# A two-block network on one NeuronCore: the memory loaded whole into two tiles at the outset, the input right behind it and normalised ahead of the first products, and twelve products of a constant at the very start

## The chip, the cores and the metric

The kernel runs on one core of one Trainium2 chip, and the other cores are idle. The metric is the device time of one execution in microseconds (us). Inputs lie in HBM when it starts, and the output is back in HBM when it ends.

## The reference, cut to what matters

Two network blocks run one after the other on a sequence of 256 tokens of width 1024, all in float32. The first block has a gated short convolution, an MLP, a latent attention and a second MLP; each of its norms is modulated by a shift and a scale that come from a product of a vector `c` with the large matrix `ada_w`. The second block has a recurrent and an attention mixer, a cross attention over a memory of 256 rows, and an MLP. What the change touches is the cross attention's keys and values, and the first norm of the first block:

```python
# second block, cross attention: needs the memory alone, so the kernel computes it first
mem_n = rms_norm(mem, norm_mem)           # mem [1, 256, 1024]
k = mem_n @ w_xk                          # [256, 1024] x [1024, 1024]
v = mem_n @ w_xv
# first block, first norm
mod = silu(c) @ ada_w[0] + ada_b[0]       # shift, scale, gate, ...
h = rmsnorm(x, norm_g[0, 0]) * (1 + scale) + shift
bcx = h @ conv_in_w                       # [256, 1024] x [1024, 3072]
```

## The kernel before, in words

**How a product is made.** Every float32 operand is split in a high part (`hi`, rounded by ScalarE to the format that TensorE multiplies in one pass) and a low part (`lo = x - hi`, by VectorE). One logical product is three TensorE products: high by high, high by low, low by high (`mm3`, lines 236 to 238, with the weights stationary and 256 tokens moving; `mm3t`, lines 243 to 245, with the tokens stationary and 512 columns moving). Weights come in pieces of 512 KB, 128 x 1024 floats. `load` (line 212) fetches one by SyncE's DMA queue into one of 7 buffers of the pool `raw`; `split` (lines 216 and 217) makes `whi` on ScalarE and `wlo` on VectorE, after which the buffer is free again. So a load can be issued only when VectorE is done with the piece seven loads before it.

**Modulations as background.** `ada_step(n)` (line 331) loads 512 KB of the transposed `ada_w`, also into a `raw` buffer, and multiplies it on VectorE with the row `cb` (silu of `c`, spread over the partitions by eight transposes and two ScalarE copies, lines 305 and 306), summing along the row. Each `split` calls `background()`, which hands out such steps at a fixed rate for the stage. The first stage has 16 of these steps and four calls of `first_h` (lines 650 to 660), which make the modulated input `h` of the first block, two of its eight feature tiles a call.

**The first stage** (lines 591 to 687) computes the keys and values of the memory, so that TensorE has work while the modulations of the first block are made:

- For each of four quarters of the memory: load 256 KB of the transposed memory into `memT`, a tile of the pool `tmp` (7 tiles, which `memg` and `sqm` also use), load a piece of `w_xk` (lines 598, 599), scale the memory by the norm's gain into `memg` (line 602, two ScalarE copies of 128 x 256), split `memg` into `hmh` and `hml`, split the weights, and square the memory into `sqm` for the norm (line 606), added up on VectorE in `sqs` (lines 612, 614).
- The first half of the keys: 96 products of 256 columns into two PSUM tiles `us` (lines 615 to 621). Then the sums of squares by float32 products with a constant tile `ones` (`fmm`, line 248), the reciprocal roots `rm` and `rmc` (lines 626 to 634), and `memK` (line 639).
- The input `x`: two loads of 512 KB (line 678), and `first_x` (lines 662 to 670) for each 128 tokens: squares on ScalarE, `rstd`, two scaled copies `xs`, eight transposes on TensorE (line 669), two copies to `xn`. `first_h` reads `xn`.
- The second half of the keys (`up`, line 681), 96 products of 256 columns; then the values in two halves (lines 682 to 687), each 48 products of 512 columns and two ScalarE evacuations `memV`.

Then the convolution's input product begins, with `h` as its moving operand and pieces of `conv_in_w`.

**What sets the order.** The order of instructions on each engine and on SyncE's DMA queue is fixed when the program is built, by a list scheduler that goes by the order of the code and by its own estimate of when operands are there. On the chip each engine runs its list strictly in order, and waits where an operand isn't there yet.

Of the kernel before, what the change touches and what calls it, by code (L numbers as in the profile page):

```python
# [12 lines left out]
AF = mybir.ActivationFunctionType  # L13
# [22 lines left out]
TAIL = 6  # L36

# [49 lines left out]
def net(ctx, tc, t, out):  # L87
# [30 lines left out]
    def tmp(name, *shp):  # L118
        return shaped(tmpp.tile([P, 512], F32, name=name, tag="t"), shp)
# [203 lines left out]
    nc.sync.dma_start(ident, t["consts"][:, :128])  # L323
    cb = row(cact)
# [269 lines left out]
    mem, ws, sqa = [], [], None  # L594
    gm = vcol("norm_mem_2", 0, 8)
    for i in range(4):
        v = tmp("memT", 2, S)
        nc.sync.dma_start(v, t["memT"][i])
        raw = load(t["w_xk_2"][i])
        vg = tmp("memg", 2, S)  # L600
        for j in range(2):
            nc.scalar.activation(vg[:, j, :], v[:, j, :], AF.Copy, scale=gm[:, 2 * i + j:2 * i + j + 1])
        split_into(hm.ks(0, 2 * i, 2), hm.ks(1, 2 * i, 2), vg)
        ws.append(split(raw, 2, 512))
        q = tmp("sqm", 2, S)
        nc.scalar.activation(q, v, AF.Square)
        if i == 0:
            sqa = q
        else:
            if i == 1:  # L610
                sqs = big("sqs", 2, S)
                nc.vector.tensor_add(sqs, sqa, q)
            else:
                nc.vector.tensor_add(sqs, sqs, q)
    us = [utile() for _ in range(2)]
# [30 lines left out]
    xn = [big("xn", 4, S) for _ in range(2)]  # L646
# [15 lines left out]
    def first_x(tt):  # L662
        r = x_rstd(tt)
        for hf in range(2):
            v = tmp("xs", 512)
            nc.scalar.activation(v, xt[tt][:, hf, :], AF.Copy, scale=r)
            m = mtile()
            for j in range(4):
                nc.tensor.transpose(m[:, j * P:(j + 1) * P], v[:, j * P:(j + 1) * P], ident)
            nc.scalar.activation(xn[hf][:, :, tok(tt)], shaped(m, [4, P]), AF.Copy)  # L670

    for j in range(0, KT, 2):
        for n in (8 + j, j, 9 + j, j + 1):
            steps.append(((0, 0), lambda n=n: ada_step(n)))
        steps.append(((0, 0), lambda j=j: first_h(j)))
    pace["rate"] = len(steps) / MEM_PIECES
    for tt in range(2):
        nc.sync.dma_start(xt[tt], t["x"][tt * P:(tt + 1) * P, :].rearrange("p (a b) -> p a b", a=2))
    for tt in range(2):
        first_x(tt)  # L680
# [638 lines left out]
```

## Time and profile before

| | |
|---|---|
| median of 3 runs | 1044.45 us |
| lowest and highest | 1042.36 and 1044.8 us |
| the profiled execution's own time | 1044.24 us |
| its span | 1042.4 us |
| TensorE busy (matmul) | 998.4 us, 96% |
| VectorE busy | 735.2 us, 71% |
| ScalarE busy | 564.2 us, 54% |
| DMA | 231 MB, 222 GB/s mean |

The span is that of the instructions; the execution's own time holds 1.84 us more, around it. All times within the profile count from the start of the span. "PE" is TensorE, "PEld" its weight loads, "DVE" VectorE, "ACT" ScalarE, "SPq" SyncE's queue of DMA issues. A row of the timeline gives start, length, engine, line and operation, output and inputs, a count, and in brackets how long the engine had been idle just before and what ended that wait; rows of one kind that follow each other are merged. A row of products may overlap the next one, since products are pipelined: their pace is read from start to start.

### The profile page before, as it was taken

Reading aid. Unit: us, or ns where it says so; the run is one execution under the profiler, and the core shown is the slowest. Engines: PE = TensorE matmul, PEld = TensorE weight load, DVE = VectorE, ACT = ScalarE, POOL = GpSimd, SP = SyncE. Lnnn points to the kernel's source line nnn. Section 1 sums busy time; section 2 is a strip of 40 time slices with the busy share of each in tenths; the row PEclk is TensorE's granted clock in tenths of the full one; section 3 lists DMA queues with packets and bytes.
Section 4 is the critical chain, followed back from the end, with each engine's and each line's share of the span. In section 5 each row is a group of like instructions: output and inputs, shape, how many; then the busy total and the mean of one; then the engine's idle time right before and its main releaser. Section 6 shows DMA issues by size and latency. Waiting matters only on the chain.

```text
span 1042.4 us, 15822 instructions
## 1 busy us (share of the span) xinstructions
PE 998.4 (96%) x6090; PEld 871.8 (84%) x6090; DVE 735.2 (71%) x1108; ACT 564.2 (54%) x920; POOL 1.0 (0%) x8
## 2 busy tenths in 40 slices
PE   6979989999999979989999999999999999999997
PEld 5869977898888768667999988898878888998886
DVE  6878996898888589938866553868767556655542
ACT  6644446744435683868544453755556446444442
POOL 0000000000000000000000000000000000000000
PEclk9989989999999999998999999999999999999999
DMA  9788994798989369904976564573434336566611
GB/s 345 283 316 310 340 362 165 278 379 335 339 306 358 118 205 348 312 26 173 331 237 208 184 185 157 182 241 119 122 102 167 137 129 225 187 187 184 193 49 41
DMA packets 64731, 231.00 MB, mean 222 GB/s; under 512 B 7184, under 2 KB 7568, under 8 KB 64656
## 3 DMA queue, kind: packets, MB, share of 16 engines
q1 hardware_dynamic: 64512, 229.86, 63.3%
q8 instruction: 48, 0.79, 0.3%
q14 instruction: 27, 0.22, 0.1%
q10 hardware_dynamic: 144, 0.12, 0.0%
HBM read 228.91 MB, written 1.05 MB: 221 GB/s over the span
## 4 chain that ended last, share of the span: by engine, by line
PE 84%; DVE 6%; ACT 6%; DMA 2%; issue 1%; SPq 0%; ACTq 0%
PE acc L243 11%; PE acc L244 11%; PE acc L245 11%; PE u L236 10%; PE u L237 10%; PE u L238 10%; PE u L245 4%; PE u L244 4%; PE u L243 4%; PE m L248 3%; DVE wlo L217 2%; DVE raw L331 2%; ACT whi L216 1%; PE u L248 1%; PE acc L248 1%
## 5 line engine op out<-in xcount | busy, mean ns | idle before, releaser
L217 DVE TENSOR_TENSOR wlo<-raw,whi 128x1024 fp32r<-128x1024 f32 (+1 forms) x317 | 380.4, 1212 | 150.9 <-ACT whi L216 148.3
L216 ACT ACTIVATE whi<-raw 128x1024 fp32r<-128x1024 f32 (+1 forms) x317 | 327.7, 1048 | 225.9 <-PE u L237 89.8
L236 PE MATMUL u<-hh,whi 128*128 128x256 f32 x960 | 272.0, 283 | 2.7 <-ACT whi L216 2.7
L238 PE MATMUL u<-hh,wlo 128*128 128x256 f32 x960 | 271.8, 283 | 0.8 <-DVE wlo L217 0.8
L237 PE MATMUL u<-hl,whi 128*128 128x256 f32 x960 | 271.5, 283 | 0.0
L236 PEld LDWEIGHTS u<-hh,whi 128*128 128x128 f32 x960 | 182.0, 190 | 5.1 <-ACT whi L216 3.1
L237 PEld LDWEIGHTS u<-hl,whi 128*128 128x128 f32 x960 | 182.0, 190 | 1.9 <-issue 1.0
L238 PEld LDWEIGHTS u<-hh,wlo 128*128 128x128 f32 x960 | 181.8, 189 | 2.0 <-issue 1.0
L243 PE MATMUL acc<-whi,mh 128*128 128x512 f32 x384 | 151.7, 395 | 0.0
L244 PE MATMUL acc<-whi,ml 128*128 128x512 f32 x384 | 151.4, 394 | 0.0
L245 PE MATMUL acc<-wlo,mh 128*128 128x512 f32 x384 | 151.3, 394 | 0.0
L331 DVE SCALAR_TENSOR_TENSOR raw<-raw,row 128x1024 f32<-128x1024 f32 x112 | 136.1, 1219 | 5.5 <-DMA raw<-in_adaT_dram 5.4
L245 PEld LDWEIGHTS acc<-wlo,mh 128*128 128x128 f32 x384 | 72.3, 188 | 16.7
L244 PEld LDWEIGHTS acc<-whi,ml 128*128 128x128 f32 x384 | 72.3, 188 | 15.7
L243 PEld LDWEIGHTS acc<-whi,mh 128*128 128x128 f32 x384 | 72.2, 188 | 15.7
L243 PE MATMUL u<-whi,hh 128*128 128x512 f32 x144 | 59.5, 413 | 4.9 <-ACT hh L454 4.9
L244 PE MATMUL u<-whi,hl 128*128 128x512 f32 x144 | 59.4, 413 | 0.5 <-DVE hl L455 0.4
L245 PE MATMUL u<-wlo,hh 128*128 128x512 f32 x144 | 58.4, 406 | 0.0
L513 ACT ACTIVATE rl<-u 128x512 f32<-128x512 f32 x36 | 21.1, 586 | 35.1 <-PE u L238 35.1
L243 PEld LDWEIGHTS u<-whi,hh 128*128 128x128 f32 x144 | 27.9, 194 | 11.8 <-ACT hh L454 5.6
L475 DVE TENSOR_TENSOR rq<-rl 128x512 f32<-128x512 f32 x36 | 24.7, 686 | 14.3 <-ACT rl L513 14.2
L244 PEld LDWEIGHTS u<-whi,hl 128*128 128x128 f32 x144 | 28.1, 195 | 7.2 <-DVE hl L455 1.3
(318 smaller groups left out, 1241.3 us busy)
## 6 DMA issues: line engine op xcount, KB each, us to landing
raw<-in_adaT_dram SPq DMA_DIRECT2D x112, 512.0 KB, 5.4
raw<-in_mlp_up_w_dram SPq DMA_DIRECT2D x64, 512.0 KB, 5.1
raw<-in_mlp_down_w_dram SPq DMA_DIRECT2D x64, 512.0 KB, 4.7
raw<-in_w_ff_dram SPq DMA_DIRECT2D x64, 512.0 KB, 3.6
raw<-in_w_in_dram SPq DMA_DIRECT2D x28, 512.0 KB, 3.8
raw<-in_conv_in_w_dram SPq DMA_DIRECT2D x24, 512.0 KB, 4.9
raw<-in_w_xk_dram SPq DMA_DIRECT2D x8, 512.0 KB, 7.8
raw<-in_w_xv_dram SPq DMA_DIRECT2D x8, 512.0 KB, 5.7
```

The source lines that it names most:

```text
L216: nc.scalar.activation(hi, view, AF.Copy)
L217: nc.vector.tensor_sub(lo, view, f32(hi))
L236: nc.tensor.matmul(o, wh, xh, start=start, stop=False, skip_group_check=True)
L237: nc.tensor.matmul(o, wh, xl, start=False, stop=False, skip_group_check=True)
L238: nc.tensor.matmul(o, wl, xh, start=False, stop=stop, skip_group_check=True)
L243: nc.tensor.matmul(o, xh, wh, start=start, stop=False, skip_group_check=True)
L244: nc.tensor.matmul(o, xl, wh, start=False, stop=False, skip_group_check=True)
L245: nc.tensor.matmul(o, xh, wl, start=False, stop=stop, skip_group_check=True)
L248: nc.tensor.matmul(o, a, b, start=start, stop=stop, skip_group_check=True)
L331: nc.vector.scalar_tensor_tensor(raw, raw, 1.0, cb, op0=OP.mult, op1=OP.mult, accum_out=mods[:, n:n + 1])
L475: nc.vector.tensor_mul(q, h_, h_)
L513: nc.scalar.activation(r, pair(u), AF.Relu)
```

## The change

The memory gets two tiles of its own in the pool `bigp` (21 tiles of 128 x 1032 floats), half of it in each. Its four loads and those of the first four pieces of `w_xk` are issued in the code right after that of `ident`. Next in the code stand twelve float32 products of `ones` by itself, 128 x 128, into a PSUM tile that nothing reads; then the row `cb`. In the first stage the two loads of `x` stand ahead of everything, and `first_x` ahead of the first products of the keys. The gain is applied straight into `hmh` by ScalarE (two copies of 128 x 256 a quarter), and the low part is one VectorE instruction for each 128 x 256, (memory x gain) - high; `memg` is gone. The list `first_ada` gives the modulation steps in the same order as before.

```diff
+WARM = 12
...
     nc.sync.dma_start(ident, t["consts"][:, :128])
+    memt = [big("memT", 4, S) for _ in range(2)]
+    memv = [memt[i // 2][:, 2 * (i % 2):2 * (i % 2) + 2, :] for i in range(4)]
+    raws = []
+    for i in range(4):
+        nc.sync.dma_start(memv[i], t["memT"][i])
+        raws.append(load(t["w_xk_2"][i]))
+    warm = atile(3)
+    for i in range(WARM):
+        fmm(warm[:, :P], ones, ones, True, True)
     cb = row(cact)
...
+    first_ada = [n for j in range(0, KT, 2) for n in (8 + j, j, 9 + j, j + 1)]
+    for tt in range(2):
+        nc.sync.dma_start(xt[tt], t["x"][tt * P:(tt + 1) * P, :].rearrange("p (a b) -> p a b", a=2))
+    ws, sqa = [], None
     gm = vcol("norm_mem_2", 0, 8)
     for i in range(4):
-        v = tmp("memT", 2, S)
-        nc.sync.dma_start(v, t["memT"][i])
-        raw = load(t["w_xk_2"][i])
-        vg = tmp("memg", 2, S)
+        v = memv[i]
         for j in range(2):
-            nc.scalar.activation(vg[:, j, :], v[:, j, :], AF.Copy, scale=gm[:, 2 * i + j:2 * i + j + 1])
-        split_into(hm.ks(0, 2 * i, 2), hm.ks(1, 2 * i, 2), vg)
-        ws.append(split(raw, 2, 512))
+            k = 2 * i + j
+            nc.scalar.activation(hm.k(0, k), v[:, j, :], AF.Copy, scale=gm[:, k:k + 1])
+            nc.vector.scalar_tensor_tensor(hm.k(1, k), v[:, j, :], gm[:, k:k + 1], f32(hm.k(0, k)),
+                                           op0=OP.mult, op1=OP.subtract)
+        ws.append(split(raws[i], 2, 512))
...
+    xn = [big("xn", 4, S) for _ in range(2)]
+
+    def first_x(tt):
...
+    for tt in range(2):
+        first_x(tt)
     us = [utile() for _ in range(2)]
...
-    for tt in range(2):
-        nc.sync.dma_start(xt[tt], t["x"][tt * P:(tt + 1) * P, :].rearrange("p (a b) -> p a b", a=2))
-    for tt in range(2):
-        first_x(tt)
     up([t["w_xk_2"][4 + i] for i in range(4)], hm, memk_evac(1))
```

## Rows read from the trace of the kernel before

**Rows 1.** Part 1 of the page (busy time, share of the span, instructions of TensorE).
```profile
PE 998.4 (96%) x6090; PEld 871.8 (84%) x6090; DVE 735.2 (71%) x1108; ACT 564.2 (54%) x920; POOL 1.0 (0%) x8
```
**Rows 2.** Windows: for each stretch its length, then busy time and instructions of PE, PEld, DVE, ACT and POOL, the granted clock as a share of full speed, the DMA engines' share and GB/s.
```profile
50.00:60.00 10.00, 8.22 (x27) 5.96 (x28) 8.57 (x14) 6.66 (x9) 0.00 (x0) 0.83 1.02 399
60.00:80.00 20.00, 16.54 (x95) 14.66 (x94) 13.63 (x23) 8.31 (x12) 0.00 (x0) 0.91 0.81 284
76.00:140.00 64.00, 64.00 (x545) 63.90 (x544) 58.92 (x90) 29.09 (x37) 0.00 (x0) 1.00 0.92 332
```
**Rows 3.** Timeline of TensorE up to the first product of the values: the transposes of `c`, then products of the keys.
```profile
4.12 1.97 PE L305 MATMUL m<-ident,cact 128*128 128x128 f32 x8 [4.12 <-DVE cact L322]
10.30 0.80 PE L236 MATMUL u<-hmh,whi 128*128 128x256 f32 x2 [4.22 <-ACT hmh L216]
...
11.97 0.41 PE L237 MATMUL u<-hml,whi 128*128 128x256 f32 x1
...
14.10 0.40 PE L236 MATMUL u<-hmh,whi 128*128 128x256 f32 x1
...
19.59 0.39 PE L237 MATMUL u<-hml,whi 128*128 128x256 f32 x1 [0.84 <-DVE hml L217]
...
26.92 0.36 PE L236 MATMUL u<-hmh,whi 128*128 128x256 f32 x1
27.12 0.28 PE L237 MATMUL u<-hml,whi 128*128 128x256 f32 x1
...
32.70 0.28 PE L236 MATMUL u<-hmh,whi 128*128 128x256 f32 x1
...
40.18 0.39 PE L243 MATMUL u<-whi,hmh 128*128 128x512 f32 x1
```
**Rows 4.** Timeline of ScalarE and VectorE at the outset: the two halves of the first split of weights.
```profile
8.19 1.06 ACT L216 ACTIVATE whi<-raw 128x1024 fp32r<-128x1024 f32 x1 [2.71 <-DMA raw<-in_w_xk_dram]
9.28 1.23 DVE L217 TENSOR_TENSOR wlo<-raw,whi 128x1024 fp32r<-128x1024 f32 x1 [5.21 <-ACT whi L216]
```
**Rows 5.** Timeline of SyncE's queue: the four loads of the memory (the first, third and fourth), the two of `x`, and the first load for the second half of the values; then, from the view of line 678, the time from issue to landing of the loads of `x`.
```profile
1.17 0.42 SPq L598 DMA_DIRECT2D memT<-in_memT_dram  x1
...
5.41 0.66 SPq L598 DMA_DIRECT2D memT<-in_memT_dram  x1
...
13.53 0.33 SPq L598 DMA_DIRECT2D memT<-in_memT_dram  x1
...
18.75 0.90 SPq L678 DMA_DIRECT2D x<-in_x_dram  x2
...
45.16 0.33 SPq L212 DMA_DIRECT2D raw<-in_w_xv_dram  x1
...
DMA to landing us min/median/max: 6.7/7.1/7.5
```
**Rows 6.** The chain of waits, merged: the two groups of float32 products by `ones` that stand between the two halves of the keys (start, length, what).
```profile
22.71 0.96 PE m L248 x4
...
26.27 0.79 PE m L248 x8
```
**Rows 7.** Timeline of TensorE: the first of those groups, two products of 256 columns in four records.
```profile
22.57 1.10 PE L248 MATMUL m<-sqs,ones 128*128 128x256 f32 x4
```
**Rows 8.** Groups by line with shapes kept apart, from the start to 70 us: total and mean time of ScalarE's gain copies and of the memory's high and low parts; then, from VectorE's timeline, four instructions of the kind that the change brings (128 x 256).
```profile
L602 ACT ACTIVATE memg<-memT,vec 128x256 f32<-128x256 f32 x8 | 3.6, 503 | 0.6 <-DMA memT<-in_memT_dram 0.6
L217 DVE TENSOR_TENSOR hml<-memg,hmh 128x512 fp32r<-128x512 f32 x4 | 2.7, 685 | 0.0
L216 ACT ACTIVATE hmh<-memg 128x512 fp32r<-128x512 f32 x4 | 2.5, 623 | 0.0
...
91.41 1.67 DVE L717 SCALAR_TENSOR_TENSOR cg<-upad,vec,cg 128x256 f32<-128x256 f32 x4
```
**Rows 9.** Windows, columns as in rows 2: the stretch from the first memory copy to the start of `first_x`, and that of `first_x`.
```profile
4.00:28.45 24.45, 19.21 (x129) 18.01 (x130) 17.68 (x26) 17.49 (x31) 0.00 (x0) 1.00 1.00 387
28.45:39.07 10.62, 10.62 (x93) 10.60 (x92) 6.51 (x16) 9.30 (x23) 0.00 (x0) 1.00 0.85 316
```
**Rows 10.** Timelines of ScalarE and VectorE around `first_x`: its first square; the split of weights that stands behind most of it on ScalarE; VectorE's wait for that split, and its wait for the last product of the keys.
```profile
28.45 0.61 ACT L372 ACTIVATE sq<-x 128x512 f32<-128x512 f32 x1
37.05 1.04 ACT L216 ACTIVATE whi<-raw 128x1024 fp32r<-128x1024 f32 x1
38.13 1.23 DVE L217 TENSOR_TENSOR wlo<-raw,whi 128x1024 fp32r<-128x1024 f32 x1 [3.34 <-ACT whi L216]
40.38 0.69 DVE L639 TENSOR_TENSOR memK<-u,rm 128x512 f32<-128x512 f32 x1 [1.02 <-PE u L238]
```
**Rows 11.** Timeline of TensorE: the first transposes of `x`, the gap between the two halves of the values, a product some time after it, and the first product of the convolution.
```profile
32.81 0.60 PE L669 MATMUL m<-ident,xs 128*128 128x128 f32 x4
...
53.82 0.50 PE L243 MATMUL u<-whi,hmh 128*128 128x512 f32 x1 [1.72 <-ACT whi L216]
...
56.35 0.63 PE L245 MATMUL u<-wlo,hmh 128*128 128x512 f32 x1
...
66.74 0.40 PE L245 MATMUL u<-wlo,hmh 128*128 128x512 f32 x1
69.84 0.39 PE L236 MATMUL u<-hh,whi 128*128 128x256 f32 x1 [2.70 <-ACT whi L216]
```
**Rows 12.** Timeline of VectorE: the last step of the 16 modulations (the sum that `first_h` waits for).
```profile
64.83 0.16 DVE L654 TENSOR_TENSOR mods<-mods,vec 128x2 f32<-128x2 f32 x1
```

More of the change, by code (lines that the diff above doesn't have):

```diff
@@ L593, in net @@
     memV = [big("memV", D) for _ in range(2)]
-    mem, ws, sqa = [], [], None
+    first_ada = [n for j in range(0, KT, 2) for n in (8 + j, j, 9 + j, j + 1)]
+    for tt in range(2):
+        nc.sync.dma_start(xt[tt], t["x"][tt * P:(tt + 1) * P, :].rearrange("p (a b) -> p a b", a=2))
+    ws, sqa = [], None
     gm = vcol("norm_mem_2", 0, 8)
     for i in range(4):
-        v = tmp("memT", 2, S)
-        nc.sync.dma_start(v, t["memT"][i])
-        raw = load(t["w_xk_2"][i])
-        vg = tmp("memg", 2, S)
+        v = memv[i]
         for j in range(2):
-            nc.scalar.activation(vg[:, j, :], v[:, j, :], AF.Copy, scale=gm[:, 2 * i + j:2 * i + j + 1])
-        split_into(hm.ks(0, 2 * i, 2), hm.ks(1, 2 * i, 2), vg)
-        ws.append(split(raw, 2, 512))
+            k = 2 * i + j
[3 more added lines that the diff above has]
+        ws.append(split(raws[i], 2, 512))
         q = tmp("sqm", 2, S)
@@ L614, in net @@
                 nc.vector.tensor_add(sqs, sqs, q)
+    xn = [big("xn", 4, S) for _ in range(2)]
+    def first_x(tt):
+        r = x_rstd(tt)
+        for hf in range(2):
+            v = tmp("xs", 512)
+            nc.scalar.activation(v, xt[tt][:, hf, :], AF.Copy, scale=r)
+            m = mtile()
+            for j in range(4):
+                nc.tensor.transpose(m[:, j * P:(j + 1) * P], v[:, j * P:(j + 1) * P], ident)
+            nc.scalar.activation(xn[hf][:, :, tok(tt)], shaped(m, [4, P]), AF.Copy)
+    for tt in range(2):
+        first_x(tt)
     us = [utile() for _ in range(2)]
@@ L645, in net @@
     h = H("h")
-    xn = [big("xn", 4, S) for _ in range(2)]
     ga, gb1 = col("ga", 8), col("gb1", 8)
@@ L660, in first_h @@
         split_into(h.ks(0, j, 2), h.ks(1, j, 2), v)
[L662 to L670, printed above, removed]
     for j in range(0, KT, 2):
-        for n in (8 + j, j, 9 + j, j + 1):
+        for n in first_ada[2 * j:2 * j + 4]:
             steps.append(((0, 0), lambda n=n: ada_step(n)))
```

## The prediction, made before the changed kernel was run

> **What bounds the kernel now.** I read the page's busy times first: TensorE is busy 96% of the span [rows 1], so time is won only where it idles or runs at half clock. The windows say where that is. From 76 to 140 us it is busy for all 64.00 us at clock 1.00 [rows 2], so the convolution's stage goes at TensorE's pace and whatever moves its start moves its end. Ahead of it there are four places with losses: the start, the first products, a gap near 53 us and one near 68 us, each of the last two with a drop of the clock behind it [rows 2, 11].
>
> The timeline shows the first two. The first product of the keys starts at 10.30 and waits last for the memory's high part, though the weights' high part is made from 8.19 on [rows 3, 4]. Next, starts are 0.213 us apart (ten products from 11.97 to 14.10), where they later are 0.119 apart (47 from 27.12 to 32.70) [rows 3]: the first is the pace of the 1.2 GHz level, the second that of 2.4. Before 10.30 TensorE had done only eight transposes, from 4.12 to 6.1. At 19.59 there is another wait, for the fourth quarter's low part, because its load was issued only at 13.53 [rows 3, 5]: it waited for a buffer of the pool that it shares with the scaled copies and the squares.
>
> **What this stretch costs, and what it must cost.** From the first product to the first product of the values it is 40.18 - 10.30 = 29.88 us [rows 3]. The second half of the keys with the 16 transposes of x runs without a gap from 26.92 to 40.18, 13.26 us. The first half at full pace is 96 x 0.119 = 11.4 us, and the products with the constant add 0.96 + 0.79 [rows 6]. Together 26.4 us of work, so 3.5 us are lost: about 1.5 to the low clock (from 11.2 to 14.4 us at half pace), the rest to waits for the memory's low parts.
>
> **The change, part by part.**
>
> *Memory in its own tiles, loaded first.* Its four loads no longer wait for a buffer; the third and fourth go out some 2 to 9 us earlier than at 5.41 and 13.53 [rows 5]. Only 256 KB stand ahead of the first weights, as now, so I leave their landing at 8.19 and their high part at 9.25 [rows 4]. The second, third and fourth pieces of weights get up to 768 KB more ahead of them, at 387 GB/s [rows 9] at most 2 us; they are needed 2.8 us apart (24 products x 0.119), so this stays hidden behind products. The wait at 19.59 goes.
>
> *Gain straight into the high part.* ScalarE loses four instructions of 0.62 us (2.5 us) [rows 8]. VectorE exchanges 2.7 us of four low parts for eight instructions of 128 x 256 at 0.42 us, 3.3 us: 0.6 us more [rows 8]. The high part is now ready before the weights, so the first two products go at 9.25; the third needs the weights' low part, which VectorE makes from 9.28 to 10.5 [rows 4]. The full stream thus runs from about 10.45, with two products (0.24 us) done.
>
> *Twelve products of the constant.* The nearest row is the float32 group by the same tile: two products of 256 columns in 1.10 us, records 0.24 us apart, so a product of 128 columns is about 0.24 us at full clock and 0.48 at half [rows 7]: 2.9 to 5.8 us for twelve, from about 1 us (they need only the constant) to between 4 and 7. TensorE is empty there, so they cost nothing themselves. Behind them in its queue stand the eight transposes of c, 1.97 us [rows 3], which then end at 8.8 at the latest; the row they make is first used by VectorE far behind the first splits. Without that cover, if ScalarE's copies of the row stand ahead of the first weights in its list, the first product is late by 1.1 (the two copies) to 1.7 us. In return TensorE was at work until 1 to 2 us before the first key products, instead of idle for 4.2. I take the full clock for them, a gain of 1.5 us; the other end is 0.
>
> *x earlier.* Its two loads, now issued at 18.75 [rows 5], move past four pieces of key weights and several modulation loads on SyncE's queue. Those come later by 1 MB, 2.6 us at 387 GB/s; the last key weights have more slack, since the second half starts only after 23 us. `first_x` takes ScalarE from 28.45 to 39.07 with 9.30 busy, of which 1.05 is a split, so 8.25 us [rows 9, 10]. From 4.00 to 28.45 ScalarE is busy 17.49 of 24.45 us; with the 2.5 saved 9.5 us are free [rows 8, 9]. So nearly all of it fits, and it should be done near 31 rather than 39. What it held up is seen at 37.05: a split of the values' weights ran behind it, and VectorE waited 3.34 us for that, then 1.02 us for TensorE's last key products [rows 10]. Buffers free up at VectorE's pace, so the loads for the second half of the values, issued at 45.16 [rows 5], and the last modulation at 64.83 [rows 12] hung behind those waits. Without them, less the 0.6 us added, VectorE and the queue come about 3.8 us earlier. The 16 transposes only change place and are in the 26.4 us.
>
> **The sum.** The first product of the values starts at 10.45 - 0.24 + 26.4 = 36.6 instead of 40.18: 3.6 us. VectorE and the loads gain 3.8, so the rest follows by the smaller, 3.6; the gaps at 53.82 and 69.84 stay as they are [rows 11]. What is late next is the split behind each of these gaps, made on ScalarE behind the evacuations of the values. Against the profiled execution (1044.24 us, span 1042.4) that is 1040.6, and against the median, 0.2 higher, **1040.8 us**. Unknown costs: the clock (0 instead of 1.5 us) gives 1042.4, and the row's copies up to 1.7 us.
>
> **Rivals.**
>
> *It goes better, because a gap closes.* At 53.82 TensorE had waited for a split of weights whose load went out at 45.16 [rows 5, 11], and the clock then fell: 0.83 over those ten us is 1.7 us lost [rows 2]. If loads gain more than TensorE, the 1.72 us gap closes and the clock stays: another 3.4 us, 1037.4. For it: VectorE's 3.8. Against it: the split stands behind an evacuation that itself waits for TensorE, whatever the load does.
>
> *Half of it is given back at the convolution.* TensorE ends the values at about 67.0 and the last modulation is done at 64.83 [rows 11, 12], so 2.2 us can be taken from TensorE alone. If ScalarE's work on x only delays the other splits elsewhere, VectorE wins nothing, and the gain stops there: 1042.2. For it: VectorE has 58.92 busy of 64 us later on [rows 2], so it has little to catch up with. Against it: the two waits in rows 10 are idle time.
>
> *The clock is at half for the first products all the same.* A gap of 1.72 us before 53.82 was followed by products at half pace (0.63 us long at 56.35, against 0.40 at full) [rows 11], and a gap of 1 to 2 us is what I expect before the key products. 1.5 us less, 1042.4. The Trainium skill ("TensorE: Matmul & The Clock Gate", Part 4: PE-mode transpose) states that the full clock does not engage for transposes; by that rule the eight transposes of c would not keep up what the constant's products began, and the sum would be this rival's. The trace cannot say: before the first key products came transposes and an idle stretch both.
>
> *Slower: the transposes of x hold TensorE's queue.* In the list of before, x goes out behind all eight key weights though the code has it ahead of the last four [rows 5]. If it still goes out near 18.75, it lands at 25.9; from the first square to the first transpose it is 28.45 to 32.81, 4.4 us [rows 10, 11], so TensorE could have it at 30.2. Should its list place these transposes ahead of the end of the first half, which I expect at 23.6 (10.45 + 11.4 + 1.75), it stands still for 6.6 us, and the clock falls after (1.7): 8.3 - 3.6 = 4.7 us slower, 1049. It decides from a landing of x later than 19.2 us, and ends slower than before from about 22. Against it: now nothing of x's has to wait for a buffer, and the code puts it ahead of every key product.
>
> **How the numbers follow.** A run of this kernel can tell about 0.3% from no change, 3.1 us. Chances: the forecast 0.45, a closed gap 0.14, given back 0.19, half clock 0.12, slower 0.10. The forecast lies 0.5 us under the bound of 1041.3, so I count 0.40 of its 0.45 as faster: faster 0.40 + 0.14 = 0.54; same 0.05 + 0.19 + 0.12 = 0.36; slower 0.10. The range goes from 1037.0, just beyond the closed gap, to 1046.0, which holds the two smaller gains, the late row copies and the mildest part of the slower case; it leaves out most of that case and some of the tail below, together under 0.2.
>
> **What would show it.** Right: the memory's four loads issued by 5 us and x landed before 19; the first key product before 9.6 and starts 0.12 us apart from the first few on; no wait near 19; the first product of the values at 36 to 37.5; no wait of over 1 us by VectorE for a split between 30 and 42; the second half of the values loaded from about 41.5; the convolution's first product near 66. Wrong: starts 0.21 apart in the first products, a wait of TensorE just before line 669's transposes, or a convolution that starts later than 68.

## The result, and the profile after

The changed kernel took 1038.07 us (median of 6 runs, 1036.19 to 1040.28) against 1043.83 for the kernel before on the same chip (6 runs, 1042.36 to 1044.8): a ratio of 0.995, 95% interval 0.9927 to 0.9973. Run again later it took 1038.8 (7 runs) and gave 0.995 once more, 0.9931 to 0.9968. By this ratio it is 5.2 us faster (the medians differ by 5.8), where 3.6 had been forecast. The profiled execution took 1038.09 us, its span is 1036.3.

The size came out about right, and not by the forecast's way. The front of the kernel, where all of the gain was to arise, became **slower**, by 4.6 us up to the first product of the values; the gaps at 53 and 68 us, which were to stay, **went**.

Windows of the kernel after, as in [rows 2] (length, busy time and instructions of PE, PEld, DVE, ACT, POOL, granted clock, DMA share, GB/s):

```profile
50.00:60.00 10.00, 10.00 (x45) 8.13 (x44) 7.65 (x12) 6.67 (x9) 0.00 (x0) 1.00 0.89 324
60.00:80.00 20.00, 19.97 (x140) 18.40 (x139) 17.24 (x27) 10.51 (x14) 0.00 (x0) 1.00 0.91 327
76.00:140.00 64.00, 60.84 (x514) 60.48 (x513) 60.39 (x95) 29.08 (x38) 0.00 (x0) 1.00 0.94 341
```

TensorE is now busy for all of the first and 19.97 of the 20.00 us of the second, at clock 1.00 in both, against 8.22 at 0.83 and 16.54 at 0.91 [rows 2]. The 3.16 us without work in the third row are one wait, ahead of the convolution's output product at 139.46; before, the same wait lay past this stretch (output product at 144.69). The timeline of its TensorE up to the convolution answers to [rows 3, 11]:

```profile
1.05 4.55 PE L250 MATMUL acc<-ones 128*128 128x128 f32 x24 [1.05 <-DVE ones L174]
5.43 1.04 PE L307 MATMUL m<-ident,cact 128*128 128x128 f32 x8
12.86 0.80 PE L238 MATMUL u<-hmh,whi 128*128 128x256 f32 x2 [6.38 <-ACT hmh L614]
...
17.39 0.41 PE L239 MATMUL u<-hml,whi 128*128 128x256 f32 x1
17.60 0.41 PE L240 MATMUL u<-hmh,wlo 128*128 128x256 f32 x1
...
21.26 0.60 PE L638 MATMUL m<-ident,xs 128*128 128x128 f32 x4
...
31.80 0.58 PE L238 MATMUL u<-hmh,whi 128*128 128x256 f32 x1 [1.38 <-DVE memK L667]
...
44.77 0.40 PE L245 MATMUL u<-whi,hmh 128*128 128x512 f32 x1
...
66.73 0.39 PE L247 MATMUL u<-wlo,hmh 128*128 128x512 f32 x1
66.96 0.28 PE L238 MATMUL u<-hh,whi 128*128 128x256 f32 x1
```

The first product of the keys starts at 12.86, 2.56 us later than before and 3.6 later than forecast, after 6.38 us in which TensorE had nothing, and the products then start 0.21 us apart (17.39 and 17.60), the pace of the 1.2 GHz level, up to 18.0. There is no wait near 19.59 any more and none for the transposes of `x` (21.26), but a new one of 1.38 us for `memK` at 31.80, with half pace behind it up to 35.0. The values start at 44.77 instead of 40.18. From there to the convolution's first product at 66.96 there is no bracket at all: last product of the values 66.73, next 66.96.

ScalarE's timeline at the outset shows why the keys start late:

```profile
6.86 1.06 ACT L218 ACTIVATE whi<-raw 128x1024 fp32r<-128x1024 f32 x1 [1.60 <-DMA raw<-in_w_xk_dram]
...
9.29 1.05 ACT L218 ACTIVATE whi<-raw 128x1024 fp32r<-128x1024 f32 x1
...
11.79 0.61 ACT L619 ACTIVATE sqm<-memT 128x512 f32<-128x512 f32 x1
12.31 3.29 ACT L614 ACTIVATE hmh<-memT,vec 128x256 fp32r<-128x256 f32 x8
...
27.25 1.06 ACT L639 ACTIVATE xn<-m 128x512 f32<-128x512 f32 x2
```

The weights' first high part is there at 7.9, but the memory's high part, which must be there too, stands in ScalarE's list behind two copies of the row, two more splits of weights and three squares, of which the second split and the last square are shown. The last copies of `x` are done at 28.3 (39.07 before [rows 9]). SyncE's queue: the memory's fourth load at 4.32, `x` from 5.49, the first load for the values' second half at 42.87, against 13.53, 18.75 and 45.16 [rows 5]:

```profile
4.32 0.63 SPq L330 DMA_DIRECT2D memT<-in_memT_dram  x1
...
5.49 1.69 SPq L607 DMA_DIRECT2D x<-in_x_dram  x2
...
42.87 4.50 SPq L214 DMA_DIRECT2D raw<-in_w_xv_dram  x4
```

And ScalarE where the values end, which is where a part of the gain comes from (experiments 5 and 6):

```profile
64.03 1.09 ACT L685 ACTIVATE h<-xn,mods,ga 128x256 f32<-128x256 f32 x2 [1.72 <-DVE ga L680]
65.03 1.05 ACT L218 ACTIVATE whi<-raw 128x1024 fp32r<-128x1024 f32 x1
65.98 0.62 ACT L218 ACTIVATE hh<-h 128x512 fp32r<-128x512 f32 x1
...
67.45 0.67 ACT L700 ACTIVATE memV<-u,rmc 128x512 f32<-128x512 f32 x1
```

The convolution's first split of weights (65.03) and the last split of `h` (65.98) now stand **ahead** of the last evacuation of the values (`memV`, 67.45), which needs TensorE's last product of the values. In the kernel before they stand behind it, as a second profile of that kernel shows:

```profile
66.13 0.69 ACT L687 ACTIVATE memV<-u,rmc 128x512 f32<-128x512 f32 x1 [3.27 <-PE u L245]
66.71 1.08 ACT L658 ACTIVATE h<-xn,mods,ga 128x256 f32<-128x256 f32 x2
67.69 1.04 ACT L216 ACTIVATE whi<-raw 128x1024 fp32r<-128x1024 f32 x1
68.64 0.62 ACT L216 ACTIVATE hh<-h 128x512 fp32r<-128x512 f32 x1
```

The evacuation is short, 0.69 us, but ScalarE sat idle for 3.27 us before it until TensorE had ended, and the split that TensorE needs next came behind it. So TensorE's end was waited for by ScalarE, and ScalarE's next work by TensorE: that circle is the gap.

### The profile page after: what moved, and what is told of

The parts are those of the page before. It is cut to its first block, busy times and chain, and to the rows that moved or that the text cites. A ratio compares the mean times of both kernels' runs of the same rounds, so it can differ in the third digit from the quotient of the medians.

```text
span 1036.3 us, 15870 instructions
## 1 busy us (share of the span) xinstructions
PE 998.1 (96%) x6114; PEld 873.5 (84%) x6114; DVE 736.1 (71%) x1112; ACT 562.0 (54%) x916; POOL 1.0 (0%) x8
## 4 chain that ended last, share of the span: by engine, by line
PE 87%; ACT 5%; DVE 4%; DMA 2%; issue 1%; SPq 0%; ACTq 0%; DVEq 0%
PE acc L245 11%; PE acc L246 11%; PE acc L247 11%; PE u L239 11%; PE u L238 11%; PE u L240 11%; PE u L246 4%; PE u L247 4%; PE u L245 4%; PE m L250 3%; PE u L250 1%; DVE wlo L219 1%; PE acc L250 1%; DVE raw L342 1%; ACT h L463 1%
```

## The stages of all kernels

Each experiment is named below; the columns are start of the first product of the keys, start of the first product of the values, from there to the first product of the convolution, from there to the first product of the convolution's output (the first that uses `zh`), and the start of that one, all in us of one profiled execution; then the ratio of the timed runs to those of the kernel before.

| kernel | keys | values | values to conv. | conv. to output | output | ratio (95%) |
|---|---|---|---|---|---|---|
| before | 10.30 | 40.18 | 29.66 | 74.85 | 144.69 | |
| before, again | 9.25 | 39.14 | 29.65 | 75.47 | 144.26 | 0.9994 (0.9972 to 1.0016) |
| after | 12.86 | 44.77 | 22.19 | 72.50 | 139.46 | 0.995 (0.9927 to 0.9973) |
| after, again | 12.69 | 42.91 | 22.21 | 72.49 | 137.61 | 0.995 (0.9931 to 0.9968) |
| 1: x early alone | 9.76 | 50.61 | 22.34 | 71.27 | 144.22 | 1.001 (0.9997 to 1.0023) |
| 2: memory's tiles and gain alone | 9.25 | 39.65 | 28.56 | 74.78 | 142.99 | 0.9993 (0.9978 to 1.0007) |
| 3: after, no constant | 12.93 | 43.15 | 22.19 | 72.47 | 137.81 | 0.9953 (0.9936 to 0.9969) |
| 4: after, x behind the memory | 9.47 | 47.37 | 22.25 | 72.44 | 142.06 | 1.0009 (0.9992 to 1.0027) |
| 5: before, second boundary reordered | 8.99 | 38.88 | 26.95 | 73.38 | 139.21 | 0.9969 (0.9954 to 0.9984) |
| 6: after, split held back | 13.15 | 44.87 | 24.09 | 73.73 | 142.69 | 0.9973 (0.9957 to 0.9989) |
| 7: early keys, late transposes | 10.32 | 46.37 | 22.24 | 72.18 | 140.79 | 0.9971 (0.9954 to 0.9988) |
| 8: the same, no constant | 8.27 | 44.48 | 22.24 | 72.47 | 139.19 | 0.9977 (0.9961 to 0.9992) |
| 9: before, both boundaries | 8.91 | 38.79 | 25.71 | 73.55 | 138.05 | 0.9976 (0.9962 to 0.999) |
| 10: front mended | 9.76 | 40.18 | 27.40 | 72.76 | 140.34 | 0.9962 (0.9945 to 0.9979) |

The two profiles of before agree within 0.01 us in the values' stage, and so do those of after within 0.02. Behind the output product the span goes on for 896.8 to 902.0 us in these profiles, without a pattern by kernel: two profiles of before have 897.7 and 900.4. So one execution's end says little below 3 us; the stages ahead of it say much more, and the ratios come from the timed runs.

By means of the two profiles each, after against before: 43.84 - 39.66 = 4.2 us lost up to the values, 22.2 - 29.66 = 7.5 gained in the values' stage, 72.5 - 75.16 = 2.7 gained in the convolution's: 5.9 in all, where the timed runs give 5.2 (2.8 to 7.6).

## The experiments

Three theories went through all of them: **A**, ScalarE's order at the boundaries; **B**, the forecast's sum in the front; **C**, the constant's products. Two more came up on the way: **D**, that what is won here is given back later, and **V**, that VectorE's modulations set the start of the convolution.

**1 and 2: the parts alone, in the kernel before.** The first moves the loads of `x` and `first_x` ahead of the key products and leaves the rest; the second has the memory's tiles and the gain, without the constant, with `x` where it was.

```diff
+    for tt in range(2):          # 1: ahead of the loop of the key products
+        nc.sync.dma_start(xt[tt], t["x"][tt * P:(tt + 1) * P, :].rearrange("p (a b) -> p a b", a=2))
+    for tt in range(2):
+        first_x(tt)
...
-WARM = 12                        # 2: in the changed kernel, and first_x back behind memk_evac
+WARM = 0
```

> The kernel before with one part of the change: x's loads and first_x stand ahead of the first key products; memory, gain and splits as before, no products of the constant. Theory A (ScalarE's list): what gained time is that x's preparation is gone from ScalarE when the values begin, so that splits stand ahead of the evacuations at both boundaries; then TensorE has no wait over 1 us between 40 and 75 us, the clock does not fall there, the convolution's first product comes near 66 to 67 and the time is 0.993 to 0.997 of before. Theory B (the front, my forecast's sum): the time comes from the earlier, faster first products; those are as before here, so the first product of the values stays near 40 to 42 us and the time is 0.998 to 1.000. Theory C (the constant's products): without them nothing is gained, 1.000.

> The change without its x part and without the products of the constant: memory in its own tiles and loaded first, gain straight into the high part; x's loads and first_x behind the first key products as before. Theory A: the list at both boundaries is the old one (two evacuations, then the splits), so the gaps near 53 and 68 us and the falls of the clock stay, 0.998 to 1.001. Theory B: first key product near 9.5 us, values from about 37, 0.9965 to 0.9985. Theory C: 1.000.

Measured: 1045.13 us (12 runs) and 1043.13 (12 runs), with the ratios of the table: neither alone moves the time clear of noise. Both ways of that are instructive. TensorE of the second, then of the first kernel:

```profile
9.25 0.79 PE L238 MATMUL u<-hmh,whi 128*128 128x256 f32 x2 [1.95 <-ACT hmh L612]
...
53.79 0.50 PE L245 MATMUL u<-whi,hmh 128*128 128x512 f32 x1 [1.72 <-ACT whi L218]
...
68.21 0.39 PE L238 MATMUL u<-hh,whi 128*128 128x256 f32 x1 [2.70 <-ACT whi L218]
```

```profile
30.05 1.28 PE L624 MATMUL m<-ident,xs 128*128 128x128 f32 x8 [3.65 <-ACT xs L621]
```

With the memory's part alone both gaps (1.72 and 2.70 us) stay, as A has it, and the values start at 39.65, where B expected about 37. The keys start at 9.25, to the digit of the forecast, but that is luck, as ScalarE of the second kernel shows:

```profile
7.26 1.06 ACT L218 ACTIVATE whi<-raw 128x1024 fp32r<-128x1024 f32 x1 [2.05 <-DMA raw<-in_w_xk_dram]
...
8.70 0.50 ACT L612 ACTIVATE hmh<-memT,vec 128x256 fp32r<-128x256 f32 x1
```

The weights came at 7.26 instead of 8.19, and the memory's high part stands behind their split here too, so TensorE still waited for it (the bracket at 9.25). From the start of that split to the first product it is 1.99 us, against 2.11 in before (8.19 to 10.30); before's second profile, with weights at 7.14, has its first product at 9.25 as well. So this part gave the keys about 0.1 us.

With `x` alone both gaps are gone (22.34 us from values to convolution), and TensorE stands 3.65 us for the scaled copies of `x`, then 1.39 for `memK`, and its clock is 0.57 between 30 and 40 us: the values start 10.4 us late. That is the forecast's slower rival, mechanism and place. What A expected of the boundaries was right, what it expected of the time was not.

**3 and 4: the change less one part.** The third leaves out the constant's products (`WARM = 0`); the fourth moves the two loads of `x` behind the loop that prepares the memory.

> The change with WARM = 0, all else as changed. In the changed kernel the clock is at half for its first key products although the constant's products had been run, since TensorE idles 6.4 us in between. Theory A and B: without them nothing changes, 0.994 to 0.996 of before, like the changed kernel; the transposes of c take about 2.0 instead of 1.0 us. Theory C: the gain goes, 0.999 to 1.001.

> The change with x's two loads moved in the code from ahead of the memory's high parts to behind them (still ahead of first_x and the key products). On ScalarE's list the high parts then stand behind the first split instead of behind three splits and four squares, so the first key product should come near 9.5 us instead of 12.9, at full clock if 2 to 3 us without products leave it up. Theory A: the front has slack, because VectorE and the loads set when the values and the convolution can go on; TensorE then waits again somewhere between 37 and 66 us, the convolution starts within 1.5 us of the changed kernel's 66.96, and the time is 0.993 to 0.997 of before. Theory B: 3 to 5 us more than the change, 0.990 to 0.992.

Measured: 1039.34 us (8 runs) and 1045.0 (12 runs). Without the constant the ratio is 0.9953 against 0.995, with the first products at half pace in both: C falls for this kernel. In the fourth the keys start at 9.47 instead of 12.86, so it is the place of these two loads in the code that puts `hmh` late in ScalarE's list; and TensorE then gets to the transposes before `x` does:

```profile
27.18 1.55 PE L636 MATMUL m<-ident,xs 128*128 128x128 f32 x8 [3.49 <-ACT xs L633]
```

The wait of 3.49 us and a clock of 0.59 from 30 to 40 us take back more than the early keys gave: values at 47.37. B falls here: three parts of its front are in this kernel, and it is no faster than before. So, by these rows, the changed kernel's `x` is in time for the most part because its keys are late; its `x` is also issued earlier (5.49 against 7.63) and scaled 1.3 us earlier.

**5 and 6: the boundary by itself, put in and taken out.** The fifth is the kernel before with one order forced: the last evacuation stands behind the convolution's first split and the last split of `h`, which the code makes ahead of it for this. The sixth is the changed kernel with the splits of weights forced behind that evacuation.

```diff
+    h_done = made[:]                                   # 5: the last split of h
+    conv0 = piece(t["conv_in_w"][0], KT, P)            #    and the convolution's first split
...
+    for ins in made + h_done:
+        st_.enter_context(tc.issue_after(ins))
     nc.scalar.activation(memV[tt][:, hf * 512:hf * 512 + 512], u, AF.Copy, scale=rmc[:, 2 * tt:2 * tt + 1])
...
+    hold.append(last_ev.ins)                           # 6: in the changed kernel
...
+    if hold:                                           #    in split()
+        st_.enter_context(tc.issue_after(hold.pop()))
```

> The kernel before, with one thing changed: the last evacuation of the values is put behind the convolution's first split of weights and the last split of h in ScalarE's list, the order that the changed kernel's list has by itself. Memory, x and the constant stay as before. Theory A (the gain comes from ScalarE's order where the values end): the first key product stays at 10.30, values at 40.18, the gap of 1.72 us between the halves of the values stays, but the gaps of 2.70 and 0.76 us at 69.84 go and the clock stays at 1.00 behind them; convolution's first product near 67.2 and its first evacuation 3 to 4 us earlier than 78.35; time 1040 to 1041.5, ratio 0.996 to 0.998. Theory B (the gain comes from the front: memory, gain, x): no change, 1044, ratio 0.9995 to 1.0005. Theory D (gaps here are paid back later, the time is set elsewhere): the gap goes, and the time still stays at 1043 to 1045.

> The changed kernel, with one thing changed: the splits of weights wait in ScalarE's list behind the last evacuation of the values, as in the kernel before. Theory A: TensorE waits 2 to 3 us ahead of the convolution for that split, and its clock falls after; the convolution's first product near 69.5, its first evacuation near 77 instead of 73.1; time 1041 to 1042.5, ratio to the kernel before 0.997 to 0.9985. Theory B: as the changed kernel, 1038, ratio 0.9945 to 0.9955. Theory D: the gap comes back and the time is that of the changed kernel.

Measured: 1041.7 us (12 runs) against 1045.32, and 1041.49 (12 runs). The order alone gains 0.31% (3.2 us, interval 1.7 to 4.8) with nothing of the change in the kernel, and taking it out of the changed kernel brings its ratio from 0.995 to 0.9973, 2.4 us back; the intervals of these two overlap (0.9931 to 0.9968, 0.9957 to 0.9989), so the sixth's time alone does not show it, but its profile shows the gap. ScalarE and TensorE of the fifth:

```profile
64.74 1.04 ACT L218 ACTIVATE whi<-raw 128x1024 fp32r<-128x1024 f32 x1
65.69 0.61 ACT L218 ACTIVATE hh<-h 128x512 fp32r<-128x512 f32 x1
66.20 0.66 ACT L696 ACTIVATE memV<-u,rmc 128x512 f32<-128x512 f32 x1
```

```profile
65.44 0.40 PE L247 MATMUL u<-wlo,hmh 128*128 128x512 f32 x1
65.83 0.38 PE L238 MATMUL u<-hh,whi 128*128 128x256 f32 x1
```

and of the sixth:

```profile
67.27 0.69 ACT L703 ACTIVATE memV<-u,rmc 128x512 f32<-128x512 f32 x1 [1.38 <-PE u L249]
67.86 3.89 ACT L218 ACTIVATE whi<-raw 128x1024 fp32r<-128x1024 f32 x4
```

```profile
66.85 0.39 PE L249 MATMUL u<-wlo,hmh 128*128 128x512 f32 x1
68.96 0.39 PE L240 MATMUL u<-hh,whi 128*128 128x256 f32 x1 [1.72 <-ACT whi L218]
```

In the fifth the convolution follows the values at 0.39 us, where before it was 69.84 - 66.74 = 3.10, and the clock from 60 to 80 us is 1.00 instead of 0.91 [rows 2]; in the sixth the gap is back, with a bracket of 1.72, and the clock is 0.91 there. That bracket is the evacuation and the split behind it, 0.69 + 1.04 = 1.73 us; the copies of `h` stand ahead of it in the sixth, and in before they are in the wait of 2.70 as well (1.08 us). The profile prices this boundary at 3.10 - 0.23 = 2.87 us plus some 1.8 in the convolution's stage (75.16 to 73.38); the timed runs are below that, and their interval just holds it. A is shown for this boundary, by the fifth's time and by the gap that goes and comes back with the order.

**7, 8 and 10: a better front.** The seventh takes the early keys of the fourth and holds the transposes of `x` behind the first and second piece of the second half of the keys; the eighth is the same without the constant; the tenth mends what the seventh lost.

```diff
-    for tt in range(2):                                # 7
-        first_x(tt)
+    xs = [x_scaled(tt) for tt in range(2)]
...
+    up([t["w_xk_2"][4 + i] for i in range(4)], hm, memk_evac(1), lambda n: x_turned(n, xs[n]) if n < 2 else None)
...
+        if k == KT - 2:                                # 10: sums of squares, rm and rmc here
...
+    xs = [x_scaled(0), behind(rm_done, lambda: x_scaled(1))]
```

> The changed kernel with three edits: the loads of x stand behind the memory's preparation in the code (which in an earlier run put the memory's high part early, first key product at 9.47), the transposes of x are held behind the first and the second quarter of the second half of the keys, and the first split of the convolution stands ahead of the values' last evacuation in the code. Theory A with the forecast's sum in the front: first key product 9.2 to 9.6 at full pace soon after, no wait for the scaled copies, first product of values at 36 to 38.5, no gaps at the boundaries unless VectorE is late; the convolution's first product at 62 to 65 and its first evacuation at 69 to 71.5, 2 to 4 us ahead of the changed kernel: 1034 to 1036.5, ratio 0.991 to 0.993. Theory V (VectorE's modulations, last at 63.8, hold the start of the convolution): TensorE waits ahead of the convolution for the last part of h, and the time is 1037 to 1039, ratio 0.9935 to 0.9955.

> The previous kernel without the twelve products of the constant. The forecast's step (the constant's products give the first key products the full clock, 1.5 us): the first key products are 0.21 us apart for three to four us, everything behind comes 1.3 to 1.7 us later, 1.0 to 1.7 us slower than the previous kernel if the start of the convolution follows TensorE, the same if VectorE sets it. Theory C (the constant's products do nothing): within 0.5 us of the previous kernel, and its first key products at the same pace.

> The run with early keys and late transposes, mended where it lost 7.2 us: the sums of squares are multiplied ahead of the last quarter of the first key products, the scaled copies of the second 128 tokens of x stand behind the reciprocal roots on ScalarE, and both boundaries have the order of the run with both. Theory A with the forecast's front: no wait for memK, first product of values at 36.5 to 39.5, no gaps at the boundaries, convolution's first product at 62.5 to 65: 1034.5 to 1037.5, ratio 0.990 to 0.993. Theory V (VectorE, whose last modulation has come at 62.7 to 64.6 in every variant, sets the convolution's start): a front that is 5 us earlier is handed over to a wait ahead of the convolution, its first product stays at 64.5 to 66, and the time is that of the changed kernel within 1 us, ratio 0.994 to 0.996.

Measured: 1041.92, 1042.18 and 1040.22 us (12 runs each). All three beat the kernel before, and none came below the changed one. The seventh's stall moved on; its TensorE, and the ScalarE rows behind it:

```profile
10.32 0.50 PE L240 MATMUL u<-hmh,whi 128*128 128x256 f32 x2 [3.39 <-ACT hmh L615]
...
11.06 0.29 PE L242 MATMUL u<-hmh,wlo 128*128 128x256 f32 x1
11.19 0.28 PE L240 MATMUL u<-hmh,whi 128*128 128x256 f32 x1
...
30.95 0.58 PE L240 MATMUL u<-hmh,whi 128*128 128x256 f32 x1 [7.18 <-DVE memK L676]
```

```profile
26.40 1.33 ACT L639 ACTIVATE xs<-x,rstd 128x512 f32<-128x512 f32 x2
27.64 0.45 ACT L663 ACTIVATE rm<-m,epsc 128x256 f32<-128x256 f32 x1
```

TensorE waited 7.18 us for `memK`: the reciprocal roots `rm` stood on ScalarE behind the scaled copies of `x`. In the eighth the first products were at half pace, as expected without the constant, but its wait for `memK` is 6.20 us instead of 7.18: most of what the constant had bought was lost in that wait. In the tenth that wait is gone (0.17 us), and the values start at 40.18, but a wait of 2.87 us appears at 54.52:

```profile
54.52 0.50 PE L247 MATMUL u<-whi,hmh 128*128 128x512 f32 x1 [2.87 <-ACT whi L218]
```

```profile
52.92 0.60 ACT L695 ACTIVATE h<-xn,mods,ga 128x256 f32<-128x256 f32 x1 [4.00 <-DVE mods L691]
53.42 1.04 ACT L218 ACTIVATE whi<-raw 128x1024 fp32r<-128x1024 f32 x1
```

The split of weights, which I had put there to come ahead of the evacuation, stood behind a part of `first_h` that waited 4.00 us for VectorE's modulations. The times expected first failed in the seventh and the tenth, and the loss of 1.0 to 1.7 us in the eighth. The other way, a wait for VectorE ahead of the convolution, didn't come either, in that place: the 7.18 us are ScalarE's order, and of the tenth's loss VectorE's modulations are the cause one boundary sooner.

**9: both boundaries in the kernel before.** As the fifth, and the first split for the second half of the values made ahead of the second evacuation of the first half.

> The kernel before with both boundaries reordered on ScalarE: the first split of weights for the second half of the values is made and listed ahead of the second evacuation of the first half (its load moves one modulation ahead on SyncE's queue with it), and the convolution's first split ahead of the last evacuation, as in the earlier run. Nothing else of the change. Theory A: the waits of 1.72 and 2.70 us both go and the clock is 1.00 from 50 to 80 us; convolution's first product at 64.5 to 65.8 for a first key product at 10.3 (1.3 earlier if the first loads land as early as in the run with one boundary); time 1038 to 1040, ratio 0.993 to 0.9955, that is as good as the whole change. Theory V (VectorE's modulations or the load set the second half of the values): the gap near 53 shrinks but stays, because the load goes out only when VectorE frees a buffer; time as with one boundary, ratio 0.9965 to 0.9975.

Measured: 1041.08 us (12 runs), 0.9976; the expected 0.993 to 0.9955 was missed. The profile shows the first gap cut into waits of 0.80, 0.66 and 0.39 us, and clock 1.00 from 50 to 80 us, so 1.2 us less in the values' stage than in the fifth. The timed runs don't show these, and the intervals of the fifth and ninth overlap. The three waits are 1.85 us together, no less than the 1.72 before: only the fall of the clock went. The time is that of one boundary, as V had it (0.9965 to 0.9975), though none of these waits was for a load: ScalarE's rows ahead of them waited 1.77 us for TensorE and 0.28 for VectorE.

So the order that I forced here doesn't close the first gap. ScalarE at this boundary, in before and then in after, shows a further difference:

```profile
51.21 0.69 ACT L687 ACTIVATE memV<-u,rmc 128x512 f32<-128x512 f32 x1 [1.77 <-PE u L245]
52.14 0.69 ACT L687 ACTIVATE memV<-u,rmc 128x512 f32<-128x512 f32 x1 [0.24 <-PE u L245]
52.72 1.05 ACT L216 ACTIVATE whi<-raw 128x1024 fp32r<-128x1024 f32 x1
```

```profile
50.53 0.69 ACT L700 ACTIVATE memV<-u,rmc 128x512 f32<-128x512 f32 x1 [1.65 <-PE u L247]
51.12 1.05 ACT L218 ACTIVATE whi<-raw 128x1024 fp32r<-128x1024 f32 x1
...
56.08 0.69 ACT L700 ACTIVATE memV<-u,rmc 128x512 f32<-128x512 f32 x1 [1.03 <-PE u L247]
```

In before the two evacuations of the first half, one for each 128 tokens, both become possible at its very end, 0.93 us apart. In after they are 5.55 us apart, about 24 products: TensorE finishes the first 128 tokens before it turns to the second, and the split right behind the first evacuation has these 5 us in hand. The kernels with a spacing of 5.54 to 5.59 us (after, 1, 3, 4, 6, 7, 8) have no gap here, those with 0.92 to 0.94 (before, 2, 5) have the wait of 1.72; the tenth's wait there has the other cause shown above. In the ninth the first evacuation, at 49.81, still came just ahead of the half's last product (50.30). So TensorE's own order, which the move of `x` changes as well, is a rival for this boundary, and no run tests it by itself.

**11 and 12: the two kernels again.**

> The changed kernel once more, on the chip and against the runs of before of the two kernels above, so that they can be compared with it: 1038 to 1040, ratio 0.994 to 0.9965. All theories agree here.

> The kernel before itself, for a second profile of it and for the spread of a comparison of it with itself: time 1043 to 1046, ratio 0.9985 to 1.0015. If the first profile of it started late by chance, its first split of weights starts near 6.9 instead of 8.19 and every landmark up to the convolution is 1.3 us earlier (first key product near 9.0, first product of values near 38.9, convolution's first product near 68.5). Theory A: the waits of 1.72 and 2.70 us are there again, with the clock below 1.00 behind each. If they were of that one execution alone, they are gone or under 0.5 us, and Theory A loses its ground.

Measured: 1038.8 us (7 runs) and 1044.52 (12 runs). Before's gaps are there again with the same brackets, 1.72 at 52.79 and 2.70 at 68.79, so they are the kernel's and not one execution's.

## Why the prediction was right or wrong

**Memory in its own tiles.** Right: all four loads are issued by 4.95 us and the wait at 19.59 is gone.

**Gain straight into the high part.** Wrong. The step that failed said "the high part is now ready before the weights". In no kernel was it: with the memory's part alone it stood behind the weights' split, and 9.25 came of weights that landed early; in the whole change the first product comes at 12.86. The step took ScalarE's list of before with the removed copies struck out; the list is made anew, and with the loads of `x` ahead in the code it puts the memory's high part behind three splits and three squares. The fourth experiment shows that these loads do it.

**Twelve products of the constant.** Right that they cost nothing; that they buy 1.5 us failed. They did raise the clock: the transposes of `c` behind them took 1.04 us instead of 1.97 [rows 3]. But TensorE then had 6.38 us without work, and the first key products were at half pace. Where the keys came early the effect was there in the seventh (full pace from 10.32), for 1.5 us in the fourth (full pace from 9.47, half from 10.9 to 14.3), and not in the tenth (half pace from 9.76). The time with and without them was the same twice over (0.995 and 0.9953; 0.9971 and 0.9977), but in the first pair the pace was half either way, and in the second a wait for `memK` took up most of the difference. What they would buy in a front without such a wait no run shows. The Trainium skill ("TensorE: Matmul & The Clock Gate", Part 4: PE-mode transpose) has it that the full clock does not engage for transposes. These rows differ: behind products that had raised the clock, transposes ran at the full pace, and in the seventh it was still there after them.

**x earlier.** Right on ScalarE: done at 28.3, forecast 31. VectorE gained 1.1 us at the last modulation (63.76 against 64.83; 1.9 between the second profiles), forecast 3.8; the loads for the second half of the values went out 2.3 us earlier, at 42.87.

**The sum.** 36.6 for the values was wrong by 8.2 us: 3.6 by the late keys (12.86 against 9.25); the other 4.6 are about what half pace costs from 12.86 to 18.0 (24 products, 0.213 instead of 0.119, 2.3 us), the wait for `memK` (1.4) and half pace behind it (14 products, 1.3). And "the gaps at 53.82 and 69.84 stay as they are" was the step that decided: both went, 7.5 us in the values' stage and 2.7 in the convolution's. Two errors of opposite sign left the total near the forecast: that the size came out was luck. The sentence rested on the order of [rows 11], a split behind an evacuation, which I took for given; moving `x` changed the lists, and in the first experiment, which has this move alone, both gaps are gone.

**The rivals.** The one by which a gap closes was nearest, at 1037.4. Its reason was a load that comes earlier; the shown reason is, for the second gap, ScalarE's order, and for the first it stays open between ScalarE's order and TensorE's. Against it stood "the split stands behind an evacuation that itself waits for TensorE, whatever the load does", which is the right mechanism, read as a constant. The slower rival, which holds TensorE's queue by the transposes of `x`, happened in experiments 1 and 4, with waits of 3.65 and 3.49 us and a fall of the clock; the changed kernel escapes it because its keys are late and its `x` is issued at 5.49. Half clock for the first products happened as well. The gain was not given back at the convolution: the last modulation came at 63.76, and TensorE went on from the values to the convolution without a wait.

**What stays open.** After and the ninth reach the output product at the same time (137.61 to 139.46, and 138.05), with 1038.8 and 1041.08 us in timed runs side by side. In these profiles most of the 2.3 us arise behind it, and no stage of the profiles shows where: from the output product on, two profiles of one kernel differ by as much. Nor did I take the first boundary's order, ScalarE's or TensorE's, out of the changed kernel alone, so its share of the 7.5 us is read from the profile, and which of the two closes that gap isn't shown.

## What to carry to other kernels

An evacuation that waits for the last product of a stage must not stand ahead of the work that the next stage needs first: the circle costs the length of both, and in most profiles here a drop of the clock on top. It did no harm where TensorE still had a group of 24 products in hand (after, first boundary). A change that moves one engine's work lets the scheduler write its whole list again, so the order at each later stage boundary is a term of the forecast, with a price of its own, before any duration is. And parts that each do nothing alone (1, 2) can gain together, or not, by the place of two loads in the code (after 0.995, the fourth 1.0009).

## What the runs showed of the hardware

The same length of wait didn't have the same price. TensorE's wait for `memK` was 1.38 us in after and the clock fell to 0.83 from 30 to 40 us; it was 1.44 and 1.43 us in after run again and in the third experiment, and it stayed at 1.00. After the wait of 1.72 us in before the clock fell in both profiles (0.83 from 50 to 60 us); after the same wait in the second experiment it stayed at 1.00. At the outset 3.39 us without work kept full pace (seventh), and 2.67 did not (tenth).

The granted clock of the windows does not show every stretch at half pace. From 10 to 20 us it reads 1.00 in the third experiment and 0.66 in after, and in both the first products start 0.21 us apart. It fell there only where the constant's products had raised the pace before; without them the pace from start to start is the sign to go by.

The first weights came between 6.28 and 8.19 us in these profiles, 8.19 in the first profile of before and 7.14 in its second, so a landing at the outset moves by itself as much as the forecast's smaller terms.
